# First products of a fused decoder block by halves of their columns, begun after two of four row tiles

## The chip, the cores and the metric

The kernel runs on one core of a Trainium2 chip. Five engines work side by side, each with its own queue in order: TensorE (PE; its weight loads are listed as PEld), VectorE (DVE), ScalarE (ACT), GpSimd (POOL) and SyncE (SP), which here only issues transfers. The metric is the device time of one execution in microseconds; the time before is 1937.11 us, the median of 3 runs (1936.69 to 1937.59).

## The reference

One decoder layer on an input of 1024 tokens by 1024 channels, in float32:

```
h = x + 1/2 * SwiGLU_1(rms(x) * ffn1_norm)          # D_FF = 2816
u = rms(h);  q, k, v, p, gates = u @ w_in
h = h + (sigmoid(gA) * yA + sigmoid(gB) * yB) @ w_out   # yA: dilated window attention, yB: causal pooling
h = h + 1/2 * SwiGLU_2(rms(h))
out = rms_final(h)

rms(x)  = x * rsqrt(mean(x*x) + 1e-6)
SwiGLU  = (silu(y @ w1) * (y @ w3)) @ w2
```

Only the beginning of the first half-step matters here: the norm of x, and the first products of it with the columns of w1 and w3.

## The kernel before

**Products of split numbers.** Each float32 operand of a large product is split into an upper part (rounded to the format `fp32r` by a copy on ACT) and a lower part (the rest, by a subtraction), and a product is three matmuls: upper by upper, upper by lower, lower by upper. `three` lists them in that order. `Sevens.split` (L301) makes the parts of a block of weights, `wc`: ACT the upper part (L303), POOL or DVE the lower (L306). `Rows` makes those of the activations: it transposes a row tile of 128 tokens by 512 channels with four 128-column matmuls into a PSUM bank (L381), ACT writes the upper part (L382, `xhi`), and `lower` lets DVE subtract it from the bank (L385, `xlo`).

**Seven products for eight.** The products of the SwiGLU are computed in a scheme that has seven products of half-size blocks, where the plain one has eight. `Quad` holds the four quarter blocks of two columns of weights (`a` from w1, `b` from w3); `operand(m)` makes the m-th weight operand, and `run(m)` multiplies it with the m-th sum of the activations. Product 1 takes b11, the left 512 channels of row tiles 0 to 3, product 2 takes b21, their right 512 channels; both add into the same bank. A product is `Sevens.product` (L314): four blocks of 128 channels, three matmuls each, with 512 columns (the tokens of four row tiles).

**The head.** `begin_up1` is an order written out by hand: each engine gets its instructions in the order of the lines. `load_all` queues the transfers on SP: x0 to x3, the first block of w1 (raw0), the first of w3 (raw1), x4, and so on. Then, for each row tile: `squares` (ACT, with the sum of the row, L259), `inverse` (a scale on DVE, L263, and a power of -1/2 on POOL, L264: the factor of each token), and `rows`, that is the scaling of half of the tile on DVE (`scaled_part`, L270: one instruction on two operands in SBUF) and the transposes with the upper part. The gain as a row is made by transposes (L814) and copied out by DVE, left half at L830, right half at L853. `keep_on(n)` puts n filler matmuls of 128 columns (L804) into PE's queue. In the profile the tiles are named `x` (row tile), `nst` (factors), `u_f10a`, `u_f10b`, `u_f11a`, `u_f11b` (banks of the first pairs; f1 is the half-step, 0 and 1 the pair), `wc_f10a` and so on (their split weights).

`Entry` runs the first products while the row tiles still come in: `operand(i)` splits the weights of item i, with the lower part on POOL, `product(i)` multiplies, `out(i)` takes the bank to SBUF. The items are product 1 of f10a, f10b, f11a, f11b, then product 2 of the same four. Item 0 runs after x3's left half is split, item 1 after the transposes of the right halves of x0 and x1, item 2 after those of x2 and x3. Row tiles 4 to 7 follow in `Entry.run`, and then the rest of the half-step, which the change doesn't touch.

Of the kernel before, what the change touches and what calls it, by code (L numbers as in the profile page):

```python
# [126 lines left out]
def tile_block(  # L127
# [129 lines left out]
    def squares(t, out):  # L257
        inv[t] = small.tile([P, 2], F32, tag="nst", name=f"nst_{t}")
        ac.activation(out, h[t], AF.Square, accum_out=inv[t][:, 0:1])  # L259

    def inverse(t):
        st = inv[t]
        ve.tensor_scalar(st[:, 0:1], st[:, 0:1], 1.0 / D, EPS, op0=OP.mult, op1=OP.add)  # L263
        gp.tensor_tensor(st[:, 1:2], st[:, 0:1], mhalf, op=OP.pow)  # L264
# [26 lines left out]
    class Sevens:  # L291
# [9 lines left out]
        def split(self, src, n, eng=None):  # L301
            w = self.fw.tile([P, 2, HALF], F32R, tag="wc", bufs=4, name=f"wc_{self.name}{n}")
            ac.activation(w[:, 0], src, AF.Copy)  # L303
            self.n_lo += 1
            eng = eng or (ve if self.n_lo % 3 == 0 else gp)
            eng.tensor_tensor(w[:, 1], src, w[:, 0].bitcast(F32), op=OP.subtract)  # L306
            return w

        def product(self, p, w, x, start=True):
            hi, lo = self.X[x]  # L310
            for k in range(4):
                r = slice(k * P, (k + 1) * P)
                for q, (a, b) in enumerate(three((w[:, 0, r], w[:, 1, r]), (hi[:, k, :], lo[:, k, :]))):
                    pe.matmul(p, a, b, start=(start and k == 0 and q == 0), stop=(k == 3 and q == 2),  # L314
                              skip_group_check=not start)

    ORDER = (1, 6, 2, 7, 5, 4, 3)

    class Quad:
# [8 lines left out]
            r = raws.get()  # L328
            self.a += [r[:, :HALF], r[:, HALF:]]

        def operand(self, m, eng=None):
            if not self.a or (m not in (1, 2) and len(self.a) == 2):
                self.get()
            a11, a12 = self.a[:2]
            a21, a22 = self.a[2:] or (None, None)
            n, half_tile = self.n, self.sv.half_tile
            if m == 1:
                src = a11
            elif m == 2:
                src = a12  # L340
            elif m == 4:
                src = a22
            elif m == 6:
                self.s1 = half_tile("s", f"{n}1")
                ve.tensor_tensor(self.s1, a21, a22, op=OP.add)
                self.s2 = half_tile("s", f"{n}2")
                ve.tensor_tensor(self.s2, self.s1, a11, op=OP.subtract)  # L347
                src = self.s2
            elif m == 7:
                src = half_tile("s", f"{n}3")  # L350
                ve.tensor_tensor(src, a11, a21, op=OP.subtract)
            elif m == 5:
                src = self.s1
            else:
                src = half_tile("s", f"{n}4")
                ve.tensor_tensor(src, a12, self.s2, op=OP.subtract)
            self.w[m] = self.sv.split(src, f"{n}{m}", eng)

        def run(self, m, back=True):
            if m not in self.w:  # L360
# [26 lines left out]
    class Entry:  # L387
# [3 lines left out]

        def __init__(self, sv, todo, low, more):
            self.sv, self.todo, self.low, self.more = sv, todo, low, more
            self.banks = {}

        def operand(self, i):
            if i < len(self.todo):
                self.todo[i][0].operand(self.todo[i][1], gp)

        def out(self, i):  # L400
            self.todo[i][2](self.todo[i][1], self.banks.pop(i))
# [365 lines left out]
    def load_rows(*ts):  # L767
        for t in ts:
            nc.sync.dma_start(h[t], x[t * P:(t + 1) * P, :])
# [5 lines left out]

    def load_all():
        nc.scalar.dma_start(ident, c_ident)
        load_rows(0, 1, 2, 3)
        raws.depth = 2
        raws.load()  # L780
        load_rows(4)
        raws.depth = 3
        raws.load()
        load_rows(5)
        raws.depth = 4
        raws.load()
        load_rows(6, 7)
        raws.depth = 6
        raws.load()
# [5 lines left out]
    def begin_up1():  # L795
# [31 lines left out]
        inverse(0)  # L827
        g = [gains(b) for b in range(2)]
        keep_on(2)
        ve.tensor_copy(gain_row[:, LOWS], g[0])  # L830
        squares(1, square)
        squares(2, square)
        rows(0, "b11", LOWS)
        inverse(1)
# [18 lines left out]
        ve.tensor_copy(gain_row[:, HIGHS], g[1])  # L853
# [1293 lines left out]
```

## Time and profile before

| | before |
|---|---|
| median of 3 runs | 1937.11 us (1936.69 to 1937.59) |
| profiled execution, its own time | 1938.85 us |
| its span, first to last instruction | 1937.1 us |
| granted TensorE clock, mean | 0.997 |
| PE busy over the span | 1906.0 us (98%), 8938 matmuls |
| DVE, ACT, POOL busy | 1347.7, 759.3, 741.2 us |
| first matmul of `u_f10a`, of `u_f11a` | 14.06 us, 22.54 us |

A row of the timeline gives the start in us from the first instruction, the duration, the engine, the line of the source, the operation, the tiles as output<-inputs, the shape and, in brackets, how long the engine had been idle and what released it. Several instructions of a kind in a row are merged (x4), and the duration then runs from the first start to the last end. A table of stretches gives each engine's busy time between two moments. Line numbers in the profile of before are those of the kernel before; after the change the same lines stand a little lower.

### The profile page before, as it was taken

The numbers are of one execution on the slowest core, as the hardware profiler recorded it, in microseconds if no ns is written. First come the engines' busy times: TensorE is split into PE (matmuls) and PEld (weight loads), VectorE is DVE, ScalarE is ACT, GpSimd is POOL, SyncE is SP. The second block draws the span as 40 slices with busy tenths as digits, with TensorE's granted clock in tenths as the row PEclk, the third lists the DMA queues.
The fourth block names the chain that finished last, engine by engine and source line by source line (L and its number), as shares of the span: only waits on it lengthen the run. The fifth ranks groups of instructions, "written<-read, shape, count | busy, mean of one in ns | idle before, by whom it ended". The sixth has DMA issues, their size and how long they took to land.

```text
span 1937.1 us, 24938 instructions
## 1 busy us (share of the span) xinstructions
PE 1906.0 (98%) x8938; PEld 1574.9 (81%) x8938; DVE 1347.7 (70%) x2012; ACT 759.3 (39%) x1361; POOL 741.2 (38%) x557
## 2 busy tenths in 40 slices
PE   9999999999999999999999999999999999999997
PEld 7788888887888888888877888887888888878885
DVE  7786556658676876658775896787665566577776
ACT  6333333333344543334445762353333333333343
POOL 5433333332222355445544356543333333322231
PEclk9999999999999999999999999999999999999998
DMA  4154222336465538665668877733433233364654
GB/s 187 44 195 167 90 87 104 136 114 212 146 235 208 197 99 257 219 207 198 217 232 303 279 226 248 271 133 118 165 121 114 82 105 123 121 206 136 205 199 150
DMA packets 144796, 331.98 MB, mean 171 GB/s; under 512 B 19104, under 2 KB 39840, under 8 KB 143136
## 3 DMA queue, kind: packets, MB, share of 16 engines
q1 hardware_dynamic: 137136, 308.00, 46.4%
q10 hardware_dynamic: 7536, 22.39, 3.4%
q8 instruction: 70, 1.15, 0.3%
q14 instruction: 54, 0.44, 0.1%
HBM read 229.61 MB, written 100.73 MB: 171 GB/s over the span
## 4 chain that ended last, share of the span: by engine, by line
PE 39%; DVE 4%; issue 3%; POOL 2%; ACT 2%; DMA 1%; DVEq 0%; POOLq 0%; ACTq 0%
PE d_f L708 7%; PE wo L1870 4%; PE u_mixm L314 2%; PE yp L1626 2%; PE o L1572 1%; PE u_f210a L314 1%; PE u_f29b L314 1%; PE u_f29a L314 1%; PE u_f28b L314 1%; PE u_f28a L314 1%; PE u_f27b L314 1%; PE u_f27a L314 1%; PE u_f26b L314 1%; PE u_f26a L314 1%; PE u_f25b L314 1%
## 5 line engine op out<-in xcount | busy, mean ns | idle before, releaser
L708 PE MATMUL d_f<-bhi_f,alo_f 128*128 128x512 f32 x616 | 240.8, 391 | 2.5 <-POOL alo_f L670 2.1
L708 PE MATMUL d_f<-bhi_f,ahi_f 128*128 128x512 f32 x616 | 240.6, 391 | 0.2 <-ACT ahi_f L666 0.2
L708 PE MATMUL d_f<-blo_f,ahi_f 128*128 128x512 f32 x616 | 239.7, 389 | 0.0
L670 POOL TENSOR_TENSOR alo_f<-g_f,ahi_f 128x512 fp32r<-128x512 f32 x70 | 99.0, 1430 | 299.5 <-ACT ahi_f L666 299.5
L314 PE MATMUL u_mixm<-xhi_t_mix,wc_mixm 128*128 128x512 f32 x608 | 195.3, 392 | 1.8 <-POOL wc_mixm L306 1.7
L314 PE MATMUL u_mixm<-xhi_b_mix,wc_mixm 128*128 128x512 f32 x456 | 149.1, 392 | 1.2 <-ACT y_m L972 0.9
L708 PEld LDWEIGHTS d_f<-bhi_f,alo_f 128*128 128x128 f32 x616 | 115.6, 188 | 29.6 <-POOL alo_f L670 4.0
L314 PEld LDWEIGHTS u_mixm<-xhi_t_mix,wc_mixm 128*128 128x128 f32 x608 | 113.8, 188 | 27.3 <-POOL wc_mixm L306 3.8
L708 PEld LDWEIGHTS d_f<-bhi_f,ahi_f 128*128 128x128 f32 x616 | 115.6, 188 | 24.2 <-ACT ahi_f L666 0.6
L708 PEld LDWEIGHTS d_f<-blo_f,ahi_f 128*128 128x128 f32 x616 | 115.7, 188 | 23.8
L314 PE MATMUL u_mixm<-xlo_t_mix,wc_mixm 128*128 128x512 f32 x304 | 118.4, 390 | 0.0
L306 POOL TENSOR_TENSOR wc_mixm<-s_mixm,wc_mixm 128x512 fp32r<-128x512 f32 x52 | 74.4, 1433 | 108.1 <-ACT wc_mixm L303 104.1
L314 PEld LDWEIGHTS u_mixm<-xhi_b_mix,wc_mixm 128*128 128x128 f32 x456 | 85.6, 188 | 19.5 <-ACT y_m L972 1.3
L303 ACT ACTIVATE wc_mixm<-s_mixm 128x512 fp32r<-128x512 f32 x76 | 47.3, 629 | 126.5 <-DVE s_mixm L347 63.3
L314 PE MATMUL u_mixm<-xlo_b_mix,wc_mixm 128*128 128x512 f32 x228 | 88.8, 389 | 0.0
L666 ACT ACTIVATE ahi_f<-g_f 128x1024 fp32r<-128x1024 f32 x84 | 81.9, 975 | 4.0 <-DMA g_f<-gs_f 3.9
L306 POOL TENSOR_TENSOR wc_mixm<-raw,wc_mixm 128x512 fp32r<-128x512 f32 x40 | 61.0, 1530 | 34.6 <-ACT wc_mixm L303 32.1
L666 ACT ACTIVATE bhi_f<-s_f2w 128x512 fp32r<-128x512 f32 x55 | 32.8, 627 | 97.9 <-DVE s_f2w L686 87.0
L1870 PE MATMUL wo<-w_o,o_hi 128*128 128x512 f32 x224 | 69.3, 391 | 0.0
L666 ACT ACTIVATE bhi_f<-s_f1w 128x512 fp32r<-128x512 f32 x55 | 33.0, 630 | 86.8 <-DVE s_f1w L686 82.0
L314 PEld LDWEIGHTS u_mixm<-xlo_t_mix,wc_mixm 128*128 128x128 f32 x304 | 57.1, 188 | 11.8 <-DVE xlo_t_mix L385 0.2
L670 DVE TENSOR_TENSOR alo_f<-g_f,ahi_f 128x1024 fp32r<-128x1024 f32 x42 | 51.3, 1222 | 7.3 <-ACT ahi_f L666 7.3
(1302 smaller groups left out, 5103.8 us busy)
## 6 DMA issues: line engine op xcount, KB each, us to landing
g_f<-gs_f SPq DMA_DIRECT2D x70, 512.0 KB, 4.5
gs_f<-y_f SPq DMA_DIRECT2D x88, 256.0 KB, 3.0
raw<-in_w2a_dram SPq DMA_DIRECT2D x35, 512.0 KB, 3.7
raw<-in_w2b_dram SPq DMA_DIRECT2D x35, 512.0 KB, 4.6
gs_f<-gb_f SPq DMA_DIRECT2D x46, 256.0 KB, 2.2
raw<-in_w1a_dram SPq DMA_DIRECT2D x22, 512.0 KB, 4.8
raw<-in_w3a_dram SPq DMA_DIRECT2D x22, 512.0 KB, 5.5
raw<-in_w1b_dram SPq DMA_DIRECT2D x22, 512.0 KB, 4.3
```

Of the source, the lines that this page charges most:

```text
L303: ac.activation(w[:, 0], src, AF.Copy)
L306: eng.tensor_tensor(w[:, 1], src, w[:, 0].bitcast(F32), op=OP.subtract)
L314: pe.matmul(p, a, b, start=(start and k == 0 and q == 0), stop=(k == 3 and q == 2), skip_group_check=not start)
L666: ac.activation(hi[:, c], src, AF.Copy)
L670: eng.tensor_tensor(lo[:, d], src[:, o], hi[:, d].bitcast(F32), op=OP.subtract)
L708: pe.matmul(self.banks[m][t], l, r, start=(first and q == 0), stop=(last and q == 2))
L1572: pe.matmul(p, l, r, start=(j == 0), stop=(j == end))
L1626: pe.matmul(p, a, b, start=(j == 0), stop=(j == 11))
L1870: pe.matmul(banks[m][t], l, r, start=(st == 0 and j == 0 and q == 0), stop=(st == 1 and j == 1 and q == 2))
```

## The change

Four things change, all in the head.

1. `load_all` queues raw0 after x1, ahead of x2 and x3.
2. `split` can hand its lower part back instead of issuing it (`then`), so that the caller sets its place. The first weights are split, upper and lower part, after x1's `inverse` and ahead of x2's squares; in before this stood after x2's `rows`.
3. Items 0 and 1 are multiplied by halves of their columns, `first` (the tokens of x0 and x1) and `second` (x2 and x3), by `Entry.part` and `Sevens.terms`: 24 matmuls of 256 columns in place of 12 of 512, for each item. Item 0's first half stands ahead of x2's `rows`: first upper and lower weights with `xhi`, then with `xlo`. Item 1's first half stands around x3's `rows`. Item 0's second half stands where item 0 stood, item 1's second half where item 1 stood.
4. For that, the order of the small steps changes: DVE makes x1's `nst` ahead of x0's scaling; the lower parts of x0 and x1 both ahead of x2's scaling (in before x1's stood behind it); x2's lower part ahead of x3's scaling (in before behind it). Two of the six calls of `keep_on` go, with five filler matmuls.

```diff
         def product(self, p, w, x, start=True):
-            hi, lo = self.X[x]
             for k in range(4):
-                r = slice(k * P, (k + 1) * P)
-                for q, (a, b) in enumerate(three((w[:, 0, r], w[:, 1, r]), (hi[:, k, :], lo[:, k, :]))):
-                    pe.matmul(p, a, b, start=(start and k == 0 and q == 0), stop=(k == 3 and q == 2),
-                              skip_group_check=not start)
+                self.terms(p, w, x, k, range(3), start)
+
+        def terms(self, p, w, x, k, which, start=True, c=slice(0, HALF)):
+            (hi, lo), r = self.X[x], slice(k * P, (k + 1) * P)
+            all_of = three((w[:, 0, r], w[:, 1, r]), (hi[:, k, c], lo[:, k, c]))
+            for q in which:
+                pe.matmul(p[:, c], *all_of[q], start=(start and k == 0 and q == 0 and not c.start), stop=(k == 3 and q == 2),
+                          skip_group_check=not start or c != slice(0, HALF))
...
+        def part(self, i, c, which):
+            if i not in self.banks:
+                self.begun[i] = self.todo[i][0].begin()
+                self.banks[i] = self.begun[i][0]
+            for k in range(4):
+                self.sv.terms(*self.begun[i], "b11", k, which, c=c)
...
-        load_rows(0, 1, 2, 3)
+        load_rows(0, 1)
+        raws.depth = 1
+        raws.load()
+        load_rows(2, 3)
...
         ve.tensor_copy(gain_row[:, LOWS], g[0])
         squares(1, square)
-        squares(2, square)
-        rows(0, "b11", LOWS)
         inverse(1)
-        keep_on(2)
-        inverse(2)
-        squares(3, square)
-        rows(1, "b11", LOWS)
-        r[0].lower()
-        keep_on(3)
-        rows(2, "b11", LOWS)
-        inverse(3)
-        r[1].lower()
-        keep_on(3)
...
-        entry.operand(0)
-        rows(3, "b11", LOWS)
-        r[2].lower()
-        keep_on(2)
-        r[3].lower()
-        ve.tensor_copy(gain_row[:, HIGHS], g[1])
-        entry.product(0)
-        entry.operand(1)
+        entry.operand(0, lowers)
+        lowers.pop()()
+        squares(2, square)
+        rows(0, "b11", LOWS)
+        keep_on(2)
+        rows(1, "b11", LOWS)
+        inverse(2)
+        keep_on(3)
+        for t in (0, 1):
+            r[t].lower()
+        squares(3, square)
+        entry.part(0, first, (0, 2))
+        entry.part(0, first, (1,))
+        entry.operand(1, lowers)
+        rows(2, "b11", LOWS)
+        inverse(3)
+        lowers.pop()()
+        r[2].lower()
+        entry.part(1, first, (0, 1))
+        rows(3, "b11", LOWS)
+        entry.part(1, first, (2,))
+        r[3].lower()
+        ve.tensor_copy(gain_row[:, HIGHS], g[1])
+        entry.part(0, second, range(3))
...
-        entry.product(1)
+        entry.part(1, second, range(3))
```

More of the change, by code (lines that the diff above doesn't have):

```diff
@@ L329, in get, with operand @@
             self.a += [r[:, :HALF], r[:, HALF:]]
[L331 removed]
+        def operand(self, m, eng=None, then=None):
             if not self.a or (m not in (1, 2) and len(self.a) == 2):
@@ L356, in operand, with begin @@
                 ve.tensor_tensor(src, a12, self.s2, op=OP.subtract)
-            self.w[m] = self.sv.split(src, f"{n}{m}", eng)
+            self.w[m] = self.sv.split(src, f"{n}{m}", eng, then)
+        def begin(self):
+            self.bank["x"] = bank("mm", f"u_{self.sv.name}{self.n}1")
+            return self.bank["x"], self.w.pop(1)
         def run(self, m, back=True):
@@ L847, in begin_up1 @@
                         pairs[0], h[:4])
-        entry.operand(0)
+        lowers = []
+        first, second = slice(0, 2 * P), slice(2 * P, HALF)
+        ve.tensor_copy(gain_row[:, LOWS], g[0])
+        squares(1, square)
+        inverse(1)
+        entry.operand(0, lowers)
[17 more added lines that the diff above has]
+        entry.part(1, first, (0, 1))
         rows(3, "b11", LOWS)
-        r[2].lower()
-        keep_on(2)
+        entry.part(1, first, (2,))
         r[3].lower()
         ve.tensor_copy(gain_row[:, HIGHS], g[1])
-        entry.product(0)
-        entry.operand(1)
+        entry.part(0, second, range(3))
         square2 = columns_tile
```

18 lines of the change are left out of this document (10 added, 8 removed).

## The prediction

> **What bounds the kernel now.** I read the table of stretches first, then each engine's instructions in order of time for the first 36 us, because the change touches nothing later. In the table the columns are PE, PEld, DVE, ACT and POOL busy with their instructions, the granted clock, the DMA share and GB/s; the stretches are cut where the first product begins (14.06), where the third begins (22.54), and around the next waits of PE (59.27 to 65.18).
>
> ```profile
> 0.00:14.06 14.06, 11.10 (x72) 10.06 (x72) 6.78 (x17) 8.82 (x16) 3.34 (x9) 1.00 0.89 343
> 14.06:22.54 8.48, 7.77 (x41) 6.18 (x41) 6.77 (x10) 4.83 (x9) 3.90 (x4) 1.00 0.93 369
> 22.54:59.27 36.73, 36.41 (x200) 30.31 (x197) 32.37 (x42) 22.21 (x43) 24.66 (x18) 1.00 0.14 44
> 59.27:65.18 5.91, 4.93 (x20) 3.34 (x21) 4.63 (x8) 2.71 (x5) 1.90 (x2) 1.00 0.00 0
> 65.18:1937.10 1871.92, 1845.84 (x8611) 1525.05 (x8609) 1297.17 (x1939) 720.72 (x1290) 707.39 (x527) 1.00 0.51 172
> ```
>
> From 22.54 on PE is busy 36.41 of 36.73 us and then 1845.84 of 1871.92, and every wait that is left hangs on work that itself hangs on PE. So the rest of the kernel is a block that moves as a whole: the change is worth what it does to the start of the third product, u_f11a, at 22.54 us. The 14.06 us ahead of the first product are a chain over four engines: squares (ACT), factor (DVE, POOL), scaling (DVE), transposes (PE), upper part (ACT), lower part (DVE), once for each of four row tiles x0 to x3.
>
> TensorE in order of time (start, us, engine, line, operation; in brackets the idle time before and its releaser):
>
> ```profile
> 14.06 0.50 PE L314 MATMUL u_f10a<-xhi_b_f,wc_f10a 128*128 128x512 f32 x1 [0.24 <-ACT xhi_b_f L382]
> ...
> 22.12 0.66 PE L381 MATMUL x_b<-ident,x 128*128 128x128 f32 x4 [0.48 <-DVE x L270]
> 22.54 0.47 PE L314 MATMUL u_f11a<-xhi_b_f,wc_f11a 128*128 128x512 f32 x1
> ...
> 25.36 0.39 PE L314 MATMUL u_f11b<-xhi_b_f,wc_f11b 128*128 128x512 f32 x1
> 25.59 0.39 PE L314 MATMUL u_f11b<-xlo_b_f,wc_f11b 128*128 128x512 f32 x1
> ...
> 34.45 1.04 PE L381 MATMUL x_t<-ident,s_f1t 128*128 128x128 f32 x8
> 35.33 0.60 PE L381 MATMUL x_t<-ident,x 128*128 128x128 f32 x4
> ```
>
> What to see: u_f11a is preceded at once by the transposes of x3's right half, and these waited for its scaling on VectorE. A full matmul starts every 0.23 us (25.36, 25.59), a 128-column one, with a weight load of its own, every 0.11 us (eight from 34.45 to 35.33).
>
> ScalarE, VectorE and GpSimd:
>
> ```profile
> 5.95 1.06 ACT L259 ACTIVATE square<-x 128x1024 f32<-128x1024 f32 x1 [0.37 <-DMA x<-in_x_dram]
> 6.92 0.18 ACT L259 ACTIVATION_READ_ACCUMULATOR square<-x 128x1 f32 x1
> 7.27 1.06 ACT L259 ACTIVATE square<-x 128x1024 f32<-128x1024 f32 x1 [0.16 <-DMA x<-in_x_dram]
> 8.23 0.19 ACT L259 ACTIVATION_READ_ACCUMULATOR square<-x 128x1 f32 x1
> 9.14 0.60 ACT L382 ACTIVATE xhi_b_f<-x_b 128x512 fp32r<-128x512 f32 x1 [0.73 <-PE x_b L381]
> ...
> 12.39 0.62 ACT L303 ACTIVATE wc_f10a<-raw 128x512 fp32r<-128x512 f32 x1
> ```
>
> ```profile
> 7.64 0.75 DVE L270 SCALAR_TENSOR_TENSOR x<-x,nst,gain_ffn 128x512 f32<-128x512 f32 x1
> 8.31 0.29 DVE L263 TENSOR_SCALAR nst<-nst 128x1 f32<-128x1 f32 x2
> 9.13 0.75 DVE L270 SCALAR_TENSOR_TENSOR x<-x,nst,gain_ffn 128x512 f32<-128x512 f32 x1 [0.52 <-POOL nst L264]
> ...
> 11.90 0.74 DVE L270 SCALAR_TENSOR_TENSOR x<-x,nst,gain_ffn 128x512 f32<-128x512 f32 x1
> 12.56 0.68 DVE L385 TENSOR_TENSOR xlo_b_f<-x_b,xhi_b_f 128x512 fp32r<-128x512 f32 x1
> 14.04 0.69 DVE L385 TENSOR_TENSOR xlo_b_f<-x_b,xhi_b_f 128x512 fp32r<-128x512 f32 x1 [0.80 <-ACT xhi_b_f L382]
> 14.65 0.68 DVE L853 COPY gain_ffn<-gain 128x512 f32<-128x512 f32 x1
> 15.37 1.73 DVE L270 SCALAR_TENSOR_TENSOR x<-x,nst,gain_ffn 128x512 f32<-128x512 f32 x2
> ...
> 20.55 1.51 DVE L270 SCALAR_TENSOR_TENSOR x<-x,nst,gain_ffn 128x512 f32<-128x512 f32 x1
> ...
> 27.79 1.67 DVE L425 TENSOR_TENSOR s_f1t<-s_f1t,x 128x512 f32<-128x512 f32 x1
> ```
>
> ```profile
> 20.23 1.29 POOL L306 TENSOR_TENSOR wc_f11a<-raw,wc_f11a 128x512 fp32r<-128x512 f32 x1 [4.34 <-ACT wc_f11a L303]
> ...
> 27.17 1.74 POOL L306 TENSOR_TENSOR wc_f10b<-raw,wc_f10b 128x512 fp32r<-128x512 f32 x1
> 28.86 1.01 POOL L264 TENSOR_TENSOR nst<-nst,mhalf 128x1 f32<-128x1 f32 x1
> ```
>
> What to see: a scaling takes 0.75 us alone, but 1.51 beside POOL. The one begun at 20.55 ended at 22.06, which is 0.54 after POOL's 20.23 + 1.29 = 21.52; L425 ended at 29.46, 0.55 after POOL's 27.17 + 1.74 = 28.91; and POOL's power, begun at 28.86, ended at 29.87, 0.41 after that DVE instruction. So a DVE instruction on two operands in SBUF and a POOL instruction exclude each other: who comes second waits out the other and ends 0.55 (DVE) or 0.41 (the power) later. Lower parts read a bank (L385) and the gain copy (L853) too; they keep their 0.69 beside POOL.
>
> **The change part by part.** The chain is worked out row by row with the durations above; an instruction starts 0.03 to 0.05 after what releases it, and the next one on DVE or ACT may start about 0.1 before the end.
>
> *Loads.* The first weights are queued on SP ahead of x2 and x3. Bytes and number of issues stay. In before the third transfer released ACT at 7.27, 1.32 after the second at 5.95. The weights take that place, x2 lands at about 8.5, x3 at 9.8; the second weights keep the sixth place. ACT makes the weights' upper part at 7.27 instead of 12.39, to 7.89. x2's squares move from 7.27 to 8.5 and their sum (1.15 after the start) to 9.7; the upper part of x0, now behind them on ACT, from 9.14 to 9.6. That alone delays nothing that ends last.
>
> *x1's scaling, +0.7.* DVE now makes x1's sum ready before x0's scaling (7.64 to 8.39). POOL's power for x1 falls on that scaling and ends at 8.39 + 0.41 = 8.80. Next in POOL's queue is now the weights' lower part, ready since 7.89: it takes 8.75 to 10.04. x1's scaling gets its factor at 8.84, finds POOL in it and ends at 10.04 + 0.54 = 10.58 (before: 9.13 + 0.75 = 9.88).
>
> *The first half product.* x1's transposes run from 10.62 to 11.28 (0.66), its upper part to 11.91 (0.60), and the first matmuls of u_f10a start at 11.95 instead of 14.06. What a 256-column matmul costs no row shows: not below half a full one, 0.113, and 128 columns with their own load already go at 0.11; not above a full one, 0.227. I take 0.113, the nearest row. Eight plus four end their slots at 13.31; x1's lower part (11.93 to 12.62) is ready in time. The five filler matmuls that go stood in PE's waits for DVE: nothing.
>
> *x2 and x3, the cost.* On DVE both lower parts now stand ahead of x2's scaling, and x2's lower part ahead of x3's. x2's scaling: 12.54 to 13.29. Its transposes 13.33 to 13.99, upper part to 14.62, lower part 14.64 to 15.33, and only then x3's scaling, 15.25 to 16.00 (before: 11.90). PE has eight half matmuls of u_f10b for that time (13.78 to 14.68) and then nothing until 16.04. x3's transposes end at 16.70, upper part 17.33, lower part 18.04 (before: 14.04 + 0.69 = 14.73). u_f10a's second half starts at 17.37, its second matmul waits for 18.08, and its slots end at 19.32. The 12 half matmuls of u_f10b done early are worth 12 x 0.113 = 1.36.
>
> *The right halves.* Behind x3's lower part on DVE stand the copy of the gain (17.96 to 18.65) and the scalings of x0 and x1 (18.67 to 19.42, 19.33 to 20.08; before they ended at 17.10). Their transposes run at 19.46 and 20.12, u_f10b's second half from 20.57 to 21.93. x0's lower part comes behind its upper part (20.5 to 21.1), then x2's scaling, 21.76 to 22.51, then x1's lower part, and x3's scaling is ready at 23.03. By then POOL is in the lower part of u_f11a's weights (about 22.67 to 23.96), as it was in before at 20.23, so it ends at 24.50 (before 22.06). Transposes at 24.54, u_f11a at 24.98.
>
> *Sum.* 24.98 - 22.54 = +2.4 us. What u_f11a needs besides (weights' lower part at 23.96 for its third matmul at 25.4) is there. x4's factor and scaling move by the same 2.4, so the block behind keeps its shape. The profiled execution took 1938.85 us with a span of 1937.1; it should become 1941.3. It stands 1.74 above the median of the runs, 1937.11, so the median becomes 1939.5, that is 0.13% slower. 0.2% of the time, 3.9 us, is about what a measurement of this kernel can tell from no change.
>
> **A page's rule against a row.** Full matmuls stand 0.23 us apart although each has a weight load of its own, and eight 128-column ones 0.11 us apart. The Trainium skill says in TensorE: Matmul & The Clock Gate, Part 3, The mechanism, that a weight load overlaps running matmuls only when it targets other row groups; here all loads fill all rows. By that rule a half matmul would cost its own time and the load's: with the page's 128 columns / 1.2 GHz = 107 ns and 256 / 2.4 GHz + 2.5 = 109 ns, an estimate of 0.216, and the sum would be about +4.3. By that rule full ones would stand 0.32 apart; the trace has 0.23, so it disagrees.
>
> **The rivals.**
> 1. The lead is kept (the other side). u_f10a begins 14.06 - 11.95 = 2.1 us sooner, and if all that follows came with it the time would be 1937.1 - 2.1 = 1935.0. For it: PE does 24 half matmuls before x3 is ready. It decides if x3's scaling ends by about 12.7, as in before (11.90 + 0.74). Against it: in DVE's order that scaling stands behind x2's lower part, which hangs on PE and ACT.
> 2. Weight loads bind the half matmuls, at 0.227 each: the 48 then cost twice, part of it in PE's waits. The same chain with 0.227 brings u_f11a to 27.06: +4.5, 1941.6. It passes the 0.2% from about 0.20 each. Against it: the 0.11 of the transposes.
> 3. x1's scaling doesn't meet POOL, because the first weights land after about 8.2 or POOL comes second. Then it ends at 9.6 and the chain is 0.7 shorter: +1.75, 1938.9.
> 4. The longer waits of PE (1.4 us at 14.7, 1.5 at 23.0) cost its clock. A stretch of 3.4 us with half its time in matmuls at half speed is 1.7 more: +4.1, 1941.2. Against it: 11.10 us busy of 14.06 in before, in pieces, with 1.00 granted.
>
> **How the numbers follow.** The chain as worked out 0.72 (1938.4 to 1940.7, about 1 us either way for start delays and for who meets whom on the shared path), rival 1 0.06, rival 2 0.07, rival 3 0.10, rival 4 0.05. Predicted: 1939.5. The range takes in rival 3 with the same margin and rival 2: 1937.2 to 1941.6. Slower by over 0.2% (above 1941.0): rivals 2 and 4 and the upper tail of the chain, 0.15. Faster by over 0.2% (below 1933.2) would need more than rival 1 gives: 0.03. Within: 0.82.
>
> **What would show it.** Right: first matmul of u_f10a near 12; x1's scaling about 1.7 us long and ending after POOL's first lower part; x3's first scaling near 15.3; 128x256 matmuls 0.11 apart; u_f11a near 25. Wrong: 256-column matmuls 0.2 apart (rival 2), a scaling of x3 before x2's lower part (rival 1), a granted clock below 1.00 before 30 us (rival 4), or a wait of PE after 65 us that shrinks or grows by more than 1 us, which would break the claim that the rest moves as a block.

## The result, and the profile after

The changed kernel takes 1941.14 us in the median of 16 runs (1940.50 to 1943.29), the kernel before 1936.96 us in 16 (1935.84 to 1937.81). The ratio is 1.0022 with a 95% interval of 1.0016 to 1.0029: 4.2 us slower, against the 2.4 forecast. The time lies in the range, the sign is right, the sum is too small.

The table of stretches of the changed kernel, cut where the first product and u_f11a begin and around PE's next waits as in the prediction, and then two stretches inside the head (columns as there: PE, PEld, DVE, ACT, POOL busy, granted clock, DMA share, GB/s):

```profile
0.00:11.52 11.52, 8.46 (x54) 7.73 (x54) 5.07 (x12) 6.70 (x12) 3.18 (x8) 1.00 0.83 325
11.52:25.84 14.32, 11.05 (x73) 10.07 (x73) 9.56 (x15) 7.17 (x13) 4.10 (x4) 0.88 0.74 294
25.84:62.57 36.73, 36.34 (x200) 30.39 (x198) 32.08 (x42) 22.30 (x43) 24.68 (x18) 1.00 0.13 44
...
68.48:1939.80 1871.32, 1845.62 (x8611) 1525.26 (x8609) 1298.16 (x1939) 720.57 (x1290) 707.90 (x527) 1.00 0.49 172
...
14.45:18.04 3.59, 1.87 (x12) 1.34 (x11) 2.19 (x4) 0.60 (x1) 0.35 (x1) 1.00 1.03 411
18.04:21.45 3.41, 3.41 (x18) 3.41 (x18) 1.89 (x4) 1.34 (x3) 0.00 (x0) 0.50 1.02 401
```

The first product begins 2.5 us sooner (11.52, before 14.06) and the third, u_f11a, 3.3 us later (25.84, before 22.54). What follows keeps its length: 36.73 us to the next wait in both. New is the granted clock: 0.50 for 3.41 us, in the middle of the first two products.

TensorE of the changed kernel in order of time (start, us, engine, line, operation, idle time before and its releaser):

```profile
11.52 1.22 PE L325 MATMUL u_f10a<-xhi_b_f,wc_f10a 128*128 128x256 f32 x8
...
13.61 0.28 PE L325 MATMUL u_f10b<-xlo_b_f,wc_f10b 128*128 128x256 f32 x1
13.73 0.28 PE L325 MATMUL u_f10b<-xhi_b_f,wc_f10b 128*128 128x256 f32 x1
...
15.78 0.63 PE L397 MATMUL x_b<-ident,x 128*128 128x128 f32 x4 [1.17 <-issue]
...
17.82 0.41 PE L325 MATMUL u_f10a<-xlo_b_f,wc_f10a 128*128 128x256 f32 x1 [0.34 <-DVE xlo_b_f L401]
18.04 0.62 PE L325 MATMUL u_f10a<-xhi_b_f,wc_f10a 128*128 128x256 f32 x2
18.46 0.41 PE L325 MATMUL u_f10a<-xlo_b_f,wc_f10a 128*128 128x256 f32 x1
...
25.43 0.65 PE L397 MATMUL x_b<-ident,x 128*128 128x128 f32 x4 [1.41 <-DVE x L270]
25.84 0.47 PE L325 MATMUL u_f11a<-xhi_b_f,wc_f11a 128*128 128x512 f32 x1
```

A 256-column matmul starts 0.12 us after the one before it (13.61, 13.73); from 18.04 on it takes 0.21 (two to 18.46). PE waits 1.17 us for x3's first transposes and 1.41 for those of its right half.

VectorE, and two rows of GpSimd:

```profile
7.67 2.46 DVE L270 SCALAR_TENSOR_TENSOR x<-x,nst,gain_ffn 128x512 f32<-128x512 f32 x2
...
14.33 0.69 DVE L401 TENSOR_TENSOR xlo_b_f<-x_b,xhi_b_f 128x512 fp32r<-128x512 f32 x1 [1.41 <-ACT xhi_b_f L398]
14.94 0.74 DVE L270 SCALAR_TENSOR_TENSOR x<-x,nst,gain_ffn 128x512 f32<-128x512 f32 x1
...
23.75 1.61 DVE L270 SCALAR_TENSOR_TENSOR x<-x,nst,gain_ffn 128x512 f32<-128x512 f32 x1
```

```profile
7.71 0.56 POOL L264 TENSOR_TENSOR nst<-nst,mhalf 128x1 f32<-128x1 f32 x1 [1.22 <-DVE nst L263]
8.23 1.35 POOL L309 TENSOR_TENSOR wc_f10a<-raw,wc_f10a 128x512 fp32r<-128x512 f32 x1
```

x1's scaling, the second of the two from 7.67, ends at 10.13, 0.55 after POOL's lower part (8.23 + 1.35 = 9.58). x3's first scaling starts at 14.94, behind x2's lower part, for which DVE had waited 1.41 us; in the kernel before it started at 11.90.

### The profile page after: what moved, and what is told of

Read it like the earlier page. It is cut to its first block, busy times and chain, and to the rows that moved or that the text cites. A ratio compares the mean times of both kernels' runs of the same rounds, so it can differ in the third digit from the quotient of the medians.

```text
span 1939.8 us, 24963 instructions
## 1 busy us (share of the span) xinstructions
PE 1906.3 (98%) x8952; PEld 1576.8 (81%) x8952; DVE 1349.5 (70%) x2012; ACT 759.4 (39%) x1361; POOL 741.8 (38%) x557
## 5 line engine op out<-in xcount | busy, mean ns | idle before, releaser
L732 PEld LDWEIGHTS d_f<-bhi_f,ahi_f 128*128 128x128 f32 x616 | 115.7, 188 | 24.3 <-ACT ahi_f L690 0.6
```

The source lines that it names most:

```text
L732: pe.matmul(self.banks[m][t], l, r, start=(first and q == 0), stop=(last and q == 2))
```

## The experiments

All times stand against the kernel before, measured on the same chip in the same batch. A head is measured from x0's first transposes to u_f11a, since these transposes start between 8.3 and 9.0 us from execution to execution.

| kernel | x0's transposes | u_f11a | head | runs, median us | before, us | ratio, 95% interval |
|---|---|---|---|---|---|---|
| before, two profiles | 8.45, 8.65 | 22.54, 22.73 | 14.09, 14.08 | 11, 1937.64 | 1937.28 | 1.0001, 0.9993 to 1.0010 |
| changed, first profile | 8.49 | 25.84 | 17.35 | 16, 1941.14 | 1936.96 | 1.0022, 1.0016 to 1.0029 |
| changed, second profile | 8.54 | 24.88 | 16.34 | 11, 1941.62 | 1937.72 | 1.0024, 1.0015 to 1.0033 |
| with fillers | 8.69 | 24.91 | 16.22 | 11, 1940.43 | 1937.36 | 1.0014, 1.0005 to 1.0023 |
| order of before | 9.03 | 23.90 | 14.87 | 11, 1939.66 | 1937.36 | 1.0014, 1.0006 to 1.0023 |
| halves alone | 8.68 | 22.51 | 13.83 | 11, 1937.55 | 1937.36 | 1.0002, 0.9993 to 1.0011 |
| loads alone | 8.70 | 23.27 | 14.57 | 11, 1937.97 | 1937.36 | 1.0003, 0.9995 to 1.0012 |
| whole products | 8.79 | 28.46 | 19.67 | 8, 1942.97 | 1937.72 | 1.0027, 1.0017 to 1.0038 |
| POOL behind x2's power | 8.54 | 25.00 | 16.46 | 8, 1942.01 | 1937.72 | 1.0023, 1.0013 to 1.0033 |
| x3 ahead | 8.69 | 23.57 | 14.88 | 11, 1940.02 | 1937.88 | 1.0014, 1.0006 to 1.0023 |

**The halves alone.** In the kernel before, the first two products run as two halves each, at their old places:

```diff
-        entry.product(0)
+        for c in (slice(0, 2 * P), slice(2 * P, HALF)):
+            entry.part(0, c, range(3))
```

(the same for product 1).

> The kernel before with items 0 and 1 multiplied as two halves of 256 columns at their old places, nothing else. Theory 1: 24 half matmuls of 0.12 in place of 12 of 0.227 are 0.16 us more for each item, so +0.1 to +0.3 us. Theory 3 (the 256-column matmuls are what costs, by their weight loads): up to 2 x 12 x 0.1 = +2.4.

Head 13.83, time +0.2 us. Two rows of TensorE, the first showing the only wait inside the product:

```profile
14.66 0.50 PE L325 MATMUL u_f10a<-xhi_b_f,wc_f10a 128*128 128x256 f32 x2 [0.37 <-POOL wc_f10a L309]
...
22.51 0.47 PE L325 MATMUL u_f11a<-xhi_b_f,wc_f11a 128*128 128x512 f32 x1
```

Half matmuls cost nothing by themselves here; the rival that weight loads bind them falls.

**The loads alone.** In the kernel before, the first weights are queued ahead of x2 and x3:

```diff
-        load_rows(0, 1, 2, 3)
+        load_rows(0, 1)
+        raws.depth = 1
+        raws.load()
+        load_rows(2, 3)
```

> The kernel before with the first weights' load queued ahead of x2 and x3, nothing else: x2 and x3 land one transfer (1.3 us) later, and the split stands where it stood. My chain of rows gives x2's squares at 8.6, its scaling at 11.2 instead of 10.39, x3's at 12.7 instead of 11.90, u_f11a +0.8: median +0.8 us against before. The rival reading (the loads have slack, all of the delay comes from the order of the small steps): 0.

Head +0.48, time +0.6 us with an interval that holds zero. VectorE shows where the head's part is from:

```profile
9.81 0.15 DVE L263 TENSOR_SCALAR nst<-nst 128x1 f32<-128x1 f32 x1 [1.10 <-ACT square L259]
9.89 0.75 DVE L270 SCALAR_TENSOR_TENSOR x<-x,nst,gain_ffn 128x512 f32<-128x512 f32 x1
```

x1's scaling starts at 9.89 instead of 9.13, because in the order of before x2's sum (0.15 us) stands ahead of it on DVE, and x2 now lands 1.3 us later. In the changed kernel that sum stands behind x1's scaling, so this run doesn't say what the loads cost there.

**The order of before.** The changed kernel with loads, early weights and halves, but with the small steps of x0 to x3 on DVE and ACT in the order of before:

```diff
+        squares(3, square)
...
-        for t in (0, 1):
-            r[t].lower()
-        squares(3, square)
+        r[0].lower()
+        scaled_part(2, LOWS, gain_row)
+        inverse(3)
+        r[1].lower()
+        scaled_part(3, LOWS, gain_row)
...
-        rows(2, "b11", LOWS)
-        inverse(3)
+        r[2] = Rows(X, "b11", h[2][:, LOWS], 2)
```

> The changed kernel with the small steps in the order of before: x2's scaling behind x0's lower part, x3's behind x1's, both ahead of x2's lower part; x3's squares ahead of x1's upper part on ACT. Loads, early split and halves stay. Theory 1 (DVE's order is the delay): x2's scaling starts near 11.0 instead of 12.1, x3's near 12.5 (ending near 14.3 if it meets the second weights' lower part on POOL) instead of 14.94, and u_f11a 0.9 us sooner; the median falls by about 0.9, more if PE's waits are then too short to cost the clock (to +1.5 to +3.3 against before). Theory 2 (the clock alone): the median falls only if the stretch at 0.5 goes. Theory 3 (the halves themselves cost): no change.

Head 14.87 against 16.34 for the changed kernel, time +2.3 us, in the range of theory 1: the order of the small steps is 1.5 of the 2.26 us that the changed head is longer than before. The profiled execution, 1944.72 us, had its clock halved twice for 3.4 us (from 24.3 and from 1109.7 us), and one more run stands at 1944.19; the other nine lie between 1938.46 and 1940.65.

**x3 ahead.** The prediction's one step, with the two moves that it needs. In the changed kernel x3's first scaling goes ahead of x2's lower part, with x3's transposes ahead of the early half of u_f10b, and the second weights' split behind x2's upper part, so that POOL doesn't meet that scaling:

```diff
-        entry.operand(1, lowers)
         rows(2, "b11", LOWS)
+        entry.operand(1, lowers)
         inverse(3)
-        lowers.pop()()
+        rows(3, "b11", LOWS)
         r[2].lower()
+        lowers.pop()()
         entry.part(1, first, (0, 1))
-        rows(3, "b11", LOWS)
```

> The changed kernel with three steps moved at one place: x3's first scaling ahead of x2's lower part on DVE, x3's transposes ahead of the early half of u_f10b on PE, and the second weights' split behind x2's upper part on ACT, so that POOL's lower part doesn't meet that scaling. If the place of x3's scaling behind x2's lower part is the step that costs (the prediction's chain): x3's scaling begins near 13.6 and not near 15, its transposes near 14.5, u_f10a's second half near 16.6, u_f11a 14.8 to 15.4 us after x0's transposes (changed kernel 16.35 without its clock loss, kernel before 14.09), time +1.3 to +2.8 us against before. If the early halves and the loads cost as much by themselves: u_f11a stays above 15.8 and the time above +3.

Rows of VectorE, then of TensorE:

```profile
13.77 0.75 DVE L270 SCALAR_TENSOR_TENSOR x<-x,nst,gain_ffn 128x512 f32<-128x512 f32 x1 [0.67 <-POOL nst L264]
14.52 0.69 DVE L401 TENSOR_TENSOR xlo_b_f<-x_b,xhi_b_f 128x512 fp32r<-128x512 f32 x1
```

```profile
14.63 0.63 PE L397 MATMUL x_b<-ident,x 128*128 128x128 f32 x4 [0.78 <-PE x_b L397]
...
23.57 0.47 PE L325 MATMUL u_f11a<-xhi_b_f,wc_f11a 128*128 128x512 f32 x1
```

The scaling starts at 13.77 instead of 14.94 and the head is 14.88, in the range that the theory gave (14.8 to 15.4); the time is +2.1 us. The three moves together are 1.46 us of the head. The order of before left two of them undone (x3's transposes and the second weights' split stand there as in the changed kernel), moved other steps instead, and came to the same head, 14.87. What both have in common is x3's scaling ahead of x2's lower part. The other 0.8 us against the kernel before was not taken apart; the scaling still starts 5.08 us after x0's transposes, and 3.45 in the kernel before.

**POOL behind x2's power.** The first weights' lower part goes one place back in POOL's queue, so that x1's scaling doesn't meet it:

```diff
         entry.operand(0, lowers)
-        lowers.pop()()
...
         inverse(2)
+        lowers.pop()()
```

> The changed kernel with one instruction moved: POOL makes the lower part of the first weights behind x2's power and not ahead of it, so x1's scaling doesn't meet it. If the 0.7 us of the prediction were on the path (its third rival): x1's scaling takes 0.75 us and ends near 9.3 to 9.6, x1's transposes and the first half product begin 0.5 to 0.9 us sooner, and u_f11a comes 0.7 us sooner, time +2.5 to +3.5. If the lower part meets another scaling instead (x2's, which then ends 0.5 later): u_f11a is not sooner than in the changed kernel, but 0 to 0.6 later, time +4 to +5.

Rows of VectorE, then of TensorE:

```profile
7.72 1.43 DVE L270 SCALAR_TENSOR_TENSOR x<-x,nst,gain_ffn 128x512 f32<-128x512 f32 x2
```

```profile
11.92 1.10 PE L325 MATMUL u_f10a<-xhi_b_f,wc_f10a 128*128 128x256 f32 x7 [0.70 <-POOL wc_f10a L309]
...
13.33 0.60 PE L397 MATMUL x_b<-ident,x 128*128 128x128 f32 x4
```

The two scalings take 1.43 instead of 2.46 and x1's ends at 9.15. Nothing comes of it, by a wait that neither theory had: the half product now waits for the lower part itself (0.70 us), x2's transposes stand behind the half product on PE and start at 13.33 (changed kernel 13.06), and the head is 16.46, time +4.3 us. One wait took the place of the other.

**Whole products.** The changed kernel, with its order, loads and early weights, but with the first two products whole at their old places:

```diff
-        entry.part(0, first, (0, 2))
-        entry.part(0, first, (1,))
...
-        entry.part(0, second, range(3))
+        entry.product(0)
```

(the same for product 1).

> The changed order of the small steps, the loads and the early split stay, but the first two products run whole at their old places. What the halves give back shows alone. Theory (the order of the lower parts costs, the halves done early pay 12 x 0.113 = 1.36 us back, less what PE then waits for anyway): u_f11a 0.5 to 1.4 us later than in the changed kernel without its clock loss, that is 16.8 to 17.6 us after x0's transposes, time +3.0 to +5.0 us against before. Rival (the half matmuls themselves or their waits cost): u_f11a comes earlier than in the changed kernel, below 16.2 us after x0's transposes, and the time is nearer to before, under +2 us. Whether the clock falls here is open: PE has still longer waits, so by the theory of the clock loss it falls to 0.5 before 20 us.

Head 19.67, later than the theory's 16.8 to 17.6, which left out a loss of clock; time +5.2 us. The table of stretches:

```profile
14.00:17.00 3.00, 0.63 (x4) 0.42 (x4) 1.35 (x2) 0.85 (x2) 1.07 (x1) 1.00 1.03 411
17.00:20.00 3.00, 2.69 (x6) 1.87 (x7) 2.68 (x4) 0.81 (x2) 0.00 (x0) 0.50 1.03 411
20.00:23.00 3.00, 3.00 (x9) 2.21 (x8) 0.18 (x2) 0.59 (x2) 0.00 (x0) 0.50 0.58 225
```

Behind a stretch with PE busy 0.63 of 3 us the clock is at 0.50 for 6.83 us. The head is therefore not a price of the whole products alone: what the halves give back (1.36 by the prediction) and what they keep of the clock can't be told apart in this run. Against the changed kernel of the same batch the halves are worth 1.35 us of the median (1942.97 to 1941.62), both together.

**The changed kernel again, and with fillers.** First the changed kernel unedited; then with 13 filler matmuls in PE's three waits of the head (the profile lists each as two instructions):

```diff
         entry.part(1, first, (0, 1))
+        keep_on(5)
...
         entry.part(1, first, (2,))
+        keep_on(2)
...
             rows(t, "b21", HIGHS)
+            if t == 2:
+                keep_on(6)
             r[t - 1].lower()
```

> The changed kernel once more, unedited, beside the three that follow. If the clock loss is a property of this order (PE waiting too much between 14.4 and 17.8 us), the profile shows the granted clock at 0.5 again for about 3.4 us in the head, with u_f11a 17.2 to 17.5 us after the first transposes of x0. If the loss was an accident of one execution, the clock stays at 1.00 and u_f11a comes 16.2 to 16.5 us after x0's transposes, as it did with the fillers. Time in both cases 1940.5 to 1942.0, +3 to +4.5 us against before.

> The changed kernel with 13 filler matmuls more, in PE's three waits of the head (5 behind u_f10b's first eight half matmuls, 2 ahead of u_f10a's second half, 6 between the transposes of x2's and x3's right halves). Nothing else moves. Theory 1 (the order of the small steps is the whole delay; the granted clock of 0.5 from 18.2 to 21.7 us in the profile of after is only that one execution): the median stays at that of the changed kernel, about +4.2 us against before. Theory 2 (PE's waits cost it the clock for a stretch of 3.4 us in nearly every execution): u_f11a starts near 25.0 instead of 25.84, u_f10a's second half goes at 0.12 per matmul instead of 0.21, no stretch of the head has a granted clock below 1.00, and the median falls by 0.9 to 1.7 us, to +2.5 to +3.3 against before, with less spread than 1940.5 to 1943.3. If the fillers themselves stand in the way, up to +0.3.

The second profile of the changed kernel, the table of stretches and then TensorE:

```profile
14.45:18.04 3.59, 1.87 (x13) 1.29 (x11) 2.16 (x4) 0.60 (x2) 0.59 (x1) 1.00 1.03 411
18.04:21.45 3.41, 3.37 (x27) 3.08 (x28) 2.44 (x5) 2.06 (x5) 0.00 (x0) 1.00 1.03 405
```

```profile
8.54 0.66 PE L397 MATMUL x_b<-ident,x 128*128 128x128 f32 x4 [0.77 <-DVE x L270]
...
24.47 0.66 PE L397 MATMUL x_b<-ident,x 128*128 128x128 f32 x4 [1.29 <-DVE x L270]
24.88 0.47 PE L325 MATMUL u_f11a<-xhi_b_f,wc_f11a 128*128 128x512 f32 x1
```

The same program keeps its clock here, with the same waits of PE behind 14.5 us (1.17, 0.21 and 0.34), and its head is 16.34, 1.0 us shorter than in the first profile. So the loss comes in some executions and not in others. The runs agree: the mean granted clock was 0.996 or less in 8 of the 27 executions of the changed kernel, in 7 of the 8 with whole products, in 4 of the 30 of the order of before, x3 ahead and POOL behind x2's power, and in none of the 11 with fillers and none of the 102 of the kernel before beside these batches (all at 0.997 or 0.998). These are lower bounds, since one loss takes 1.7 of 1940 us, 0.0009, off the mean and so can hide in a reading of 0.997.

The beginning of the second profile is not that of the first. Rows of VectorE, then of ScalarE:

```profile
7.72 1.43 DVE L270 SCALAR_TENSOR_TENSOR x<-x,nst,gain_ffn 128x512 f32<-128x512 f32 x2
```

```profile
8.15 0.63 ACT L304 ACTIVATE wc_f10a<-raw 128x512 fp32r<-128x512 f32 x1 [0.97 <-DMA raw<-in_w1a_dram]
...
10.54 1.06 ACT L398 ACTIVATE xhi_b_f<-x_b 128x512 fp32r<-128x512 f32 x2
```

The first weights land at 8.15 instead of 7.29, POOL comes second, and x1's scaling ends at 9.15 without meeting it. The first half product still begins at 11.65: x2 lands later too, and the upper parts of x0 and x1 stand behind its squares on ACT until 11.60.

TensorE with the fillers:

```profile
14.64 1.28 PE L831 MATMUL idle<-ones 128*128 128x128 f32 x10
...
24.91 0.47 PE L325 MATMUL u_f11a<-xhi_b_f,wc_f11a 128*128 128x512 f32 x1
```

The wait at 14.6 is filled; the head stays what it is (16.22) and the median is +3.1 us instead of +4.2 and +3.9. That difference is not the clock alone. The executions of the changed kernel with a mean clock of 0.998, where a loss would have left 0.997 or less, have medians of 1940.72 (7 of 16) and 1941.45 (5 of 11), which is +3.8 and +3.7 against before: the clock is worth 0.2 to 0.4 us of the median. Why the fillers lie lower by more than that is not shown; they ran in another batch.

**A version built on this.** Loads and scalings as in the kernel before; the first two weights' upper parts in ACT's two waits; their lower parts on POOL behind x3's power; halves for the terms that need no lower part of the weights; and u_f11a ahead of the transposes of x2's and x3's right halves:

```diff
+        entry.part(0, first, (0,))
         entry.part(0, first, (1,))
+        rows(3, "b11", LOWS)
         r[2].lower()
+        for n in (1, 0):
+            lowers[n]()
...
+        entry.product(2)
         for t in (2, 3):
+            r[t] = Rows(X, "b21", h[t][:, HIGHS], t)
-        entry.product(2)
```

> A version built from what the runs showed: loads and the scalings of x0 to x3 in the order of before; the upper parts of the first two weights on ACT in its two waits, behind x1's and x2's upper parts; their lower parts on POOL behind x3's power, the second weights' first; the terms that need no lower part of the weights run first by halves of the columns, the rest whole; and u_f11a ahead of the transposes of x2's and x3's right halves instead of behind them. If the order of the scalings and PE's wait for x3's right half were the cost: x3's first scaling stays near 11.9 to 12.7, u_f11a begins 18.8 to 20.0 and the first product of x4's stage 1.5 to 2.7 us sooner than before, time -1.2 to -2.7 us (1934.6 to 1936.1). If half products can't pay in this head at all, because VectorE's chain ends as late anyway: within 0.7 us of before or slower.

Time 1937.86 against 1937.72, ratio 1.0002 (0.9993 to 1.0011), and not the -1.2 to -2.7 us of the first theory. Rows of TensorE, then of GpSimd:

```profile
19.34 0.39 PE L325 MATMUL u_f11a<-xhi_b_f,wc_f11a 128*128 128x512 f32 x1
...
27.72 0.73 PE L325 MATMUL u_f10a<-xhi_b_f,wc_f10a 128*128 128x512 f32 x2 [1.10 <-POOL wc_f10a L309]
```

```profile
25.91 1.75 POOL L309 TENSOR_TENSOR wc_f10a<-raw,wc_f10a 128x512 fp32r<-128x512 f32 x1 [3.39 <-PE u_f11b L325]
```

The lead is there (u_f11a at 19.34), and 1.1 us of it goes at the fifth product, which waits for the lower part of its weights. In the next version the fifth and sixth weights are split right behind the fourth:

```diff
         entry.operand(3)
         inverse(4)
+        entry.operand(4)
+        entry.operand(5)
...
-        entry.operand(4)
         entry.out(2)
-        entry.operand(5)
```

> The version before this one began u_f11a at 19.34 us, 3.2 sooner than the kernel before, and gave 1.1 to 1.5 us of it back at 26.6 us, where the fifth product waited for the lower part of its weights (POOL 25.91 to 27.66), which hung on ACT having made the upper part only at 25.20. Here the upper parts of the fifth and sixth weights are made on ACT right behind the fourth's, about 20.6 and 21.2, the lower parts on POOL at about 22.5 and 23.8. If that wait was all that stood between the gain and the rest of the kernel: no wait of PE at 26 us, the block from 30 us on stands 2.3 to 2.8 us sooner than in the kernel before, time -1.0 to -2.5 us. If another wait takes its place (x4's scaling on DVE, which now meets POOL's sixth lower part, or x4's transposes): 0.5 to 1.5 us of it are seen there and the time is within 0.7 us of before. If something behind 1800 us takes the gain (as it seemed to in that version's one profile): the lead holds to 1800 us and is gone at the end.

> The version with u_f11a ahead of the right halves and the fifth and sixth weights split early, a second time. If its gain is real: again 0.8 to 1.8 us under before, with no wait of PE over 0.3 us between 12 and 30 us and the clock at 1.00. If the first result was chance: within 0.5 us of before.

1936.59 against 1937.88 (ratio 0.9994, 0.9985 to 1.0003) and 1936.50 against 1937.28 (0.9996, 0.9987 to 1.0005). Both intervals hold 1, so the gain of 0.8 to 1.3 us is not settled by the ratio; in each batch 6 of 11 runs lie below the fastest of the 21 runs of the kernel before. TensorE in the first of them, and, for comparison, the start of the fifth product in the second profile of the kernel before:

```profile
25.92 0.39 PE L325 MATMUL u_f11b<-xhi_b_f,wc_f11b 128*128 128x512 f32 x1
26.14 0.39 PE L325 MATMUL u_f10a<-xhi_b_f,wc_f10a 128*128 128x512 f32 x1
```

```profile
28.28 0.39 PE L314 MATMUL u_f10a<-xhi_b_f,wc_f10a 128*128 128x512 f32 x1
```

The fifth product begins at 26.14 without a wait, 2.14 sooner. Only half of that is left at the end; where it goes is the next experiment.

**The kernel before again, and the end of the program.**

> The kernel before once more, unedited, as its own control: the ratio should hold 1.0000, and a second profile shows what two executions of one program differ by. If the rest of the kernel is a block that moves as a whole, the stretch from u_f11a (or the fifth product) to the last of PE's work differs from the first profile of this kernel by no more than about 1 us, and in the same places (around 1100 to 1150 and 1880 to 1905 us) where the other profiles jump against each other. If the medians of the changed versions, which lie 0.5 to 1.3 us above what their heads explain, owe that to the one profile of before that the heads were compared with: the head of this profile is 0.5 us or more shorter than 14.09 from x0's transposes to u_f11a, or its start earlier.

The head is the same to 0.01 us (14.08), so the one profile of before was no odd start. The two profiles still differ by 1.7 us in the span (1937.1, 1935.4), all of it behind 1050 us. Set side by side, instruction by instruction on ScalarE, the profiles keep their distance from that second one to within 0.5 us from the head to 1100 us (the one with fillers 0.9, the one whose clock fell at 1109.7 left out), and then part by about 1 us at a few places. One was found: a weight load near 1892 us. VectorE in the second profile of before, in the first profile of the better version, and in the second profile of the changed kernel:

```profile
1891.69 1.29 DVE L686 TENSOR_TENSOR s_f2w<-raw,raw 128x512 f32<-128x512 f32 x2 [0.22 <-DMA raw<-in_w2b_dram]
```

```profile
1890.69 1.29 DVE L710 TENSOR_TENSOR s_f2w<-raw,raw 128x512 f32<-128x512 f32 x2 [1.57 <-DMA raw<-in_w2b_dram]
```

```profile
1895.16 1.29 DVE L710 TENSOR_TENSOR s_f2w<-raw,raw 128x512 f32<-128x512 f32 x2 [1.42 <-DMA raw<-in_w2b_dram]
```

This load stands in the chain of work that ended last, in every profile. Its pieces in that chain, in the second profile of before and in the second of the changed kernel:

```profile
1886.91 4.76 DMA raw<-in_w2b_dram
```

```profile
1889.11 6.03 DMA raw<-in_w2b_dram
```

From its issue to DVE it takes 1.27 us more in the changed kernel. VectorE's wait for it is 0.22 to 0.37 us in all four profiles with the head of before (before twice, halves alone, loads alone), and 1.42 to 1.75 in seven of the ten with a changed head; in the other three (the changed kernel's first, fillers, whole products) it is 0.23 to 0.38. The load takes 4.67 to 5.25 us in the profiles with a short wait and 5.93 to 6.32 in the seven. Seven of ten against none of four may be chance; no run changed that load, and why it lands 1.2 us later is open. The kernel before has such steps too: between 1800 and 1850 us its first profile falls behind its second by 1.2 us.

## Why the prediction was right or wrong

**The chain, right from x2's scaling on.** The second profile of the changed kernel, with its clock at 1.00, follows the prediction there row by row: u_f11a was forecast at 24.98 and begins at 24.88. In the order of the chain, forecast and measured in the first and second profile: first half product 11.95, 11.52 and 11.65; x2's scaling 12.54, 12.11 and 12.35; x3's first scaling 15.25, 14.94 and 15.10; second matmul of u_f10a's second half 18.08, 17.82 and 17.98. Against the head of before the sum is +2.26 (16.34 - 14.08), forecast +2.4. The cause that it named, x3's scaling behind x2's lower part, is shown by the two versions that put that scaling ahead: 1.46 and 1.47 us of the head. That the first half product begins near the forecast in the second profile is luck in part: it came there by another path, through ACT.

**The sum, too small, and the range.** The forecast of +2.4 is a forecast of the head; the time moved by +4.2 and +3.9. A slowdown of more than 0.2%, which came (0.22%), had been given 0.15. The range reached up to 1941.6 to take in rival 2, which the runs refute; that 1941.14 lies in it is luck in that part.

**Half matmuls.** Taken at 0.113, measured 0.12. By the page's rule that the prediction weighed (the Trainium skill, TensorE: Matmul & The Clock Gate, Part 3, The mechanism) a half would have taken 0.216, by the prediction's estimate; the trace disagrees, as full matmuls already did. The 0.21 that does occur, from 18.04, is the halved clock.

**x1's scaling, right in one profile of two, and no term of its own.** In the first profile it met POOL's lower part and ended 0.55 behind it, as worked out. In the second it did not meet it, as the third rival had it (weights at 8.15, POOL second). The power for x1 met nothing in either: the prediction had it end at 8.80, 0.41 after x0's scaling; in the first profile it ran at 7.71 in 0.56 us beside the scaling that had started at 7.67. And the third rival, that the chain is then 0.7 shorter, falls twice: the heads without the meeting are 16.34 and 16.46, with it, in the profile with fillers, 16.22. Once ACT's upper parts ended as late, once the half product waited for the lower part. The +0.7 is one of several waits that end at about the same time, and taking it away uncovers the next.

**The loads.** "That alone delays nothing that ends last" fails for the loads alone (head +0.48), through x2's sum ahead of x1's scaling on DVE. In the changed order that sum stands behind, so the step did not spoil the forecast of the chain.

**Rival 4, underrated.** The loss of clock was given 0.05 and one full price, 1.7 us. It came in the first profile and, by the mean clock, in at least 3 of 10 executions. Where it came it moved u_f11a by 1.0 and not by 1.7: the ten half matmuls from 18.04 took 2.12 us instead of 1.26 and the eight transposes behind them 1.43 instead of 1.04, 1.25 together, and part of that is hidden because x0's upper part waits for x4's squares on ACT anyway. The prediction judged it by the head of before, where PE was busy 11.10 of 14.06 us with 1.00 granted. The stretch that counts is shorter: 1.87 busy of 3.59 us. Whether the loss came differed between executions of one program, and so it belonged into the sum as a share, not beside it as a case. In the median it is worth 0.2 to 0.4 us.

**"The rest moves as a block", wrong by about 1 us.** It holds to within 0.5 us up to 1050 us, with one exception. Behind that the weight load near 1892 us lands 1.2 us later in most of the profiles with a changed head. The prediction read one row for everything from 65 us to the end (PE busy 1845.84 of 1871.92, DMA share 0.51 in the mean), and took from it that no wait there hangs on anything but PE; but in the kernel before, too, the chain that ended last runs through that load there (4.76 us from 1886.91) and not through PE. The second profile of the changed kernel, without a loss of clock, shows the two terms: its span is 3.4 us longer than that of the second profile of before (1938.8, 1935.4), 2.2 up to u_f11a (24.88, 22.73) and 1.27 at that load. With 0.2 to 0.4 of clock that comes near the +3.9 and +4.2 of the medians. How many executions have the late load is not measured, so its share in the median stays open.

**Rivals 1 and 2.** The lead was not kept (u_f11a 2.3 later), and weight loads did not bind the halves (0.12).

## What to carry to other kernels

Work done early pays only if nothing that another engine waits for is put behind it: here two lower parts, each put ahead of a scaling of 0.74 us, cost more than 24 half matmuls done early could give back, and the version that kept the scalings' order and moved u_f11a instead began the fifth product 2 us sooner (its gain at the end, 0.8 to 1.3 us, is not settled). When one wait is taken from a chain, look at what the next instruction waits for before counting the gain (x1's scaling, and then the fifth weights). A matrix engine that is left half idle for some 3.5 us can lose its clock in a part of the executions, here in at least 8 of 27: cost that as a share of the runs, and look for it in more than one profile. And ask of the end of the program, by its own rows, what the chain that ends last runs through.

## What was not expected of the hardware

The clock fell to 0.50 for 3.41 us after a stretch without a long pause: in the 3.59 us ahead of it PE was busy 1.87, and no wait in it was above 1.2 us. The same stretch with the same 1.87 us left the clock at 1.00 in the next profile. The traces show what differs. In all 14 profiles the moments at which the granted clock changes lie whole multiples of 3.413 us apart (24.293, 27.706, 1109.731 and 1113.145 in the order of before, for one). Cut each profile into windows of that length that end at such moments: while the clock was at 1.00, it was halved behind every window in which PE was busy 1.45 us or less, and behind none with 1.79 or more. Of the three between, those with 1.71 and 1.74 lost it, and one with 1.65 (whole products, from 10.16) kept it. In the first profile of the changed kernel a window begins at 14.63 and takes in PE's waits; in the second, windows begin at 12.87 and at 16.28 and share them:

```profile
14.63:18.04 3.41, 1.71 (x10) 1.34 (x11) 2.01 (x4) 0.60 (x1) 0.17 (x1) 1.00 1.02 408
```

```profile
12.87:16.28 3.41, 2.24 (x19) 2.05 (x19) 1.64 (x4) 0.88 (x2) 1.81 (x2) 1.00 1.04 414
16.28:19.70 3.42, 2.86 (x21) 2.38 (x20) 2.43 (x4) 0.91 (x2) 0.00 (x0) 1.00 1.04 411
```

So the turning point lies near half of a window in these profiles, and whether this program loses its clock goes with where the windows fall against its waits, which differs from execution to execution. As an estimate from the second profile, 0.09 (turning point at 1.745) to 0.35 (at 1.785) of all positions of the windows put one of them on the wrong side; 8 of 27 executions had the low mean. In the first profile of the kernel before no position does. No run moved the windows on purpose. The Trainium skill, TensorE: Matmul & The Clock Gate, Part 1, What's actually happening, has the clock set by activity in windows of about 3.4 us that run free and don't start with the kernel; the 3.41 us and the difference between executions agree with it.

POOL's power on 128x1 ran in 0.56 us beside a DVE scaling on two operands in SBUF, while its 128x512 lower part held such a scaling up until 0.55 after its own end. In the kernel before a power had ended 0.41 behind a 128x512 DVE instruction, so the exclusion is not the same for every pair; what decides it was not tried.
